# RWKV time mixing on one core: batch 11 wholly by the DMA crossbar, stores held back between the crossbar blocks, and reordered ends

## The chip, the cores and the metric

One NeuronCore of a Trainium2 chip runs the kernel. Its engines are TensorE (PE), VectorE (DVE), ScalarE (ACT), GpSimd (POOL) and SyncE (SP), which here only issues DMAs; sixteen DMA engines move the data. The metric is device time in microseconds, lower is better.

## The reference

`x` is 16 batches x 2048 steps x 256 channels in float32. The three token-shift mixes are formed, but `k` isn't used by the output:

```python
x_prev[:, 1:, :] = x[:, :-1, :]
xv = x * time_mix_v + x_prev * (1 - time_mix_v)
xr = x * time_mix_r + x_prev * (1 - time_mix_r)
v = xv.reshape(-1, d_model) @ value_weight
r = xr.reshape(-1, d_model) @ receptance_weight
out = (1 / (1 + exp(-r)) * v).reshape(-1, d_model) @ output_weight
```

## The kernel before

The rows are cut into 64 units of 512 rows, four per batch; `g` counts units (0 to 63). Channels lie in two blocks of 128 (`ko`). Everything on the way is bf16; PSUM and the output are float32.

**Data in.** POOL's DMA queue loads a batch at a time and casts it to bf16 (`load`, L109), some five batches ahead; the last one, batch 15, is issued at `g` = 34. A batch's rows stand as 16 rows per partition, so that the row before slot `j` is slot `j - 1`, and only slot 0 needs the last slot shifted by one partition: the "wrap copy" (L408 on VectorE, in `wrap_slots`; L522 on ScalarE for the last batches). The first two batches are laid out unit by unit (`xt_first`), so there every unit has its wrap copy.

**Transposes.** The projections need channels on the partitions. For units up to 45 TensorE transposes (`transposes`, L200: eight 128 x 128 transposes a unit) and ScalarE copies PSUM to `xt` (L216). This runs up to `LOOK` = 6 units ahead of the unit that is computed (`advance`). The last `BYDMA` = 18 units are transposed by the DMA crossbar instead (`by_dma`, L181, issued on SyncE's queue): two quarters of batch 11 at `g` = `CROSS` = 40, batch 12 at 41, 13 at 43, 14 at 47 and 15 at 51. The first of these waits for the last load. Of batch 11 the units 44 and 47 are still TensorE's.

**Mixing.** The time-mix coefficients are folded into the weights, so a mix is one product and one add: `mix = c * x_prev + x`. VectorE or ScalarE forms the product of channel block 0 (`scale`, L249; `scale_act`, L491), POOL that of block 1 (`scale_pool`, L259), VectorE adds (`add`, L271). From unit 10 on a product covers two units. From `g` = `FREE` = `CROSS` on ScalarE takes block 0 of the value mix from VectorE.

**Unit g, in order.** TensorE projects receptance (`psum_r`), ScalarE takes the sigmoid to `s_sb` (L512); transposes of a later unit; TensorE projects value (`psum_v`, L279); VectorE multiplies to `z_sb` (L549); TensorE projects the output of unit `g - 1` (`psum_o`, L303), which ScalarE copies to `o_sb` (L335). From `g` = 41 (`LATE_O`) the output that is projected is that of `g - 2`, before the value. `psum_r`, `psum_v` and `psum_o` hold one buffer each, of two PSUM banks; `ps_t` has two buffers.

**Data out.** Two units are stored together, 1 MB, on SyncE's queue (`store`, L313; L338 for the first two batches), in the order in which the program names them: a store behind a crossbar transfer waits for its issue. `o_sb` and `xt` have three buffers of a batch each, `x_bf` six.

**The ends.** At the start TensorE runs 21 matmuls on zeros (L144), then the first units' transposes from float32; one-off work on weights runs beside. At the end units 60 to 62 are put out in halves (`out_part`), and `last_unit` takes unit 63 by halves and its output by quarters.

The order of issue is written out by hand: an engine runs its instructions in the program's order, and `add_manual_dep` adds a wait where data alone doesn't.

Of the kernel before, what the change touches and what calls it, by code (L numbers as in the profile page):

```python
# [15 lines left out]
def kernel(  # L16
# [38 lines left out]
    BYDMA = 4 * UB + 2  # L55
    CROSS = NU - BYDMA - LOOK
    FREE = CROSS
    LATE_O = CROSS
    START_T = [1, 3, 5, 6, 7, 9, 11, 12]
    AHEAD = 6  # L60
    PAIRS = 10
    WARM = 21
# [16 lines left out]
    late_copies = []  # L79
    x_bf = {}  # L80
# [5 lines left out]
    zeros = consts.tile([P, P], BF16)  # L86
# [13 lines left out]
    def load(b):  # L100
        if b not in x_bf:
            x_bf[b] = xpool.tile([P, J, D], BF16, name="x_bf")
        if b < BYUNIT:
            for e in range(UB):
                nc.gpsimd.dma_start(
                    out=x_bf[b][:, e * UJ : (e + 1) * UJ, :], in_=unit_rows(x, b, e)[:, 0]
                )
            return
        return nc.gpsimd.dma_start(out=x_bf[b], in_=rows(b), max_dma_last_dim=8192)  # L109
# [31 lines left out]
    def warm_up(n):  # L141
        ps = ps_t_pool.tile([P, P], FP32, name="ps_t")
        for _ in range(n):
            nc.tensor.matmul(out=ps, lhsT=zeros, rhs=zeros, start=True, stop=True)  # L144

    warm_up(WARM)

# [70 lines left out]
    def first_transposes():  # L218
        def half(h, pool, name):
            ps = pool.tile([P, UJ, KO, P], FP32, name=name)  # L220
            for jj in range(H):
                for ko in range(KO):
                    nc.tensor.transpose(
                        out=ps[:, jj, ko],
                        in_=x_unit[:, 0, h * H + jj, ko * P : (ko + 1) * P],
                        identity=ident_f,
                    )
            if h == 1:
                nc.vector.tensor_copy(out=xt[0][:, 0, :, 1:P], in_=ps[:, H - 1, :, 0 : P - 1])
            nc.scalar.copy(out=xt[0][:, 1 + h * H : 1 + h * H + H], in_=ps[:, 0:H])  # L230

        half(1, ps_r_pool, "psum_r")
        half(0, ps_v_pool, "psum_v")
# [77 lines left out]
    def store(queue, b, lo, hi):  # L311
        dst = out[b].rearrange("(p j) d -> p j d", p=P)
        queue.dma_start(out=dst[:, lo:hi, :], in_=o_sb[b][:, lo:hi, :])  # L313
# [9 lines left out]
    def output(g, z):  # L323
        b, e = divmod(g, UB)
        if e == 0:
            o_sb[b] = opool.tile([P, J, D], FP32, name="o_sb")
        j0 = e * UJ
        if g >= NU - 4:
            for h, (pool, name) in enumerate([(ps_t_pool, "ps_t"), (ps_o_pool, "psum_o")]):
                out_part(pool, name, z, b, e, h * H, H, nc.scalar.copy, nc.sync)  # L330
            return
        ps = ps_o_pool.tile([P, UJ, D], FP32, name="psum_o")
        for jj in range(UJ):
            out_matmuls(ps, z, jj, jj)
        nc.scalar.copy(out=o_sb[b][:, j0 : j0 + UJ, :], in_=ps)  # L335
        if b < BYUNIT:
            if e % 2 == 1:
                nc.sync.dma_start(  # L338
                    out=unit_rows(out, b, e - 1, 2),
                    in_=o_sb[b][:, j0 - UJ : j0 + UJ, :].rearrange("p (e j) d -> p e j d", j=UJ),  # L340
                )
        elif g >= NU - 8:
            store(nc.sync, b, j0, j0 + UJ)
        elif e % 2 == 1:
            store(nc.sync, b, j0 - UJ, j0 + UJ)

    def last_unit(g):
# [10 lines left out]
        for h, (lo, hi) in enumerate(cols):  # L358
            project(banks[h], g, 0, lo, hi)
            nc.scalar.activation(out=s_sb[:, :, lo:hi], in_=banks[h], func=ACT.Sigmoid)  # L360
        def value(h):
            lo, hi = cols[h]
            project(banks[2 + h], g, 1, lo, hi)
            nc.vector.tensor_tensor(
                out=z_sb[:, :, lo:hi], in0=s_sb[:, :, lo:hi], in1=banks[2 + h], op=ALU.mult
            )

        def before(h):
            pool, name = [(ps_o_pool, "psum_o"), (ps_r_pool, "psum_r")][h]
            out_part(pool, name, z_prev, b, e - 1, h * H, H, by_act, nc.sync)  # L370

        before(0)
        value(0)
        before(1)
        value(1)
        out_part(ps_v_pool, "psum_v", z_sb, b, e, 0, 1, by_act, nc.sync)
        out_part(ps_o_pool, "psum_o", z_sb, b, e, 1, 1, by_dve, nc.sync)
# [14 lines left out]
    def wrap_slots(piece, one=None):  # L392
# [15 lines left out]
        nc.vector.tensor_copy(  # L408
            out=xt[b][:, j, kos, 1:P], in_=xt[b][:, j + n, kos, 0 : P - 1]
        )  # L410

    tnext = 1
    last_load = None

    def advance(limit):
        nonlocal tnext, last_load
        while tnext <= min(limit, NU - 1):
# [3 lines left out]
            elif b > 1 and e == 0 and b + 5 < B:  # L421
                if b == 2:
                    load(6)
                last_load = load(b + 5)
            if tnext < NU - BYDMA:
                transposes(tnext)
# [27 lines left out]
    warm_up(WARM2)  # L454
# [44 lines left out]
    for g in range(NU - 1):  # L499
# [13 lines left out]
        if g == CROSS:  # L513
            for e in (1, 2):
                by_dma(B - 5, e * UJ, (e + 1) * UJ, last_load)
        advance(START_T[g] if g < len(START_T) else g + LOOK - (g == CROSS - 1))
        for b in range(B - 4, B):
            if g == max(UB * (b - 2) - 1, CROSS + 1):
                new_xt(b)
                by_dma(b, 0, J)  # L520
# [20 lines left out]
        for p in pooled[g]:  # L541
            wrap_slots(p)
# [6 lines left out]
        nc.vector.tensor_tensor(out=z_sb, in0=s_sb, in1=ps_v, op=ALU.mult)  # L549
        for p in pooled[g]:  # L550
            scale_pool(p, last)
# [38 lines left out]
```

## Time and profile before

| | |
|---|---|
| median of 4 runs | 203.65 us (203.1 to 204.22) |
| the profiled execution | 203.96 us, its span 202.2 us |
| TensorE, VectorE, ScalarE, POOL busy | 97%, 92%, 90%, 41% |
| DMA packets under 512 B | 19716 of 31130 |
| SyncE's queue q1, POOL's queue q0: share of 16 DMA engines | 59.3%, 40.1% |
| HBM read, written | 34.34 MB, 33.55 MB: 336 GB/s over the span |

The span runs from the first to the last recorded event; the profiled execution took 1.76 us more. An engine's busy time says how much of the span it worked, not that it set the end. A line such as L303 is a line of the kernel; a helper's line stands for all its callers, and the tile's name tells them apart. "SPq" is SyncE's queue: its time is that in which a DMA is issued, not the transfer's own.

### The profile page before, as it was taken

The page shows a single profiled execution, that of the slowest core. Times are in us where ns is not written, and L with a number is a line of the kernel's source. Part 1 is how long each engine was busy: PE and PEld are TensorE (multiplying, and loading weights), DVE is VectorE, ACT ScalarE, POOL GpSimd, SP SyncE. Part 2 cuts the span into 40 slices and gives each one's busy share as a digit, 9 for nine tenths or more (in the row PEclk, how much of TensorE's full clock was granted, in tenths as well). Part 3 has the DMA queues.
Part 4 walks back from the last instruction along what each step waited for, and adds up shares of the span by engine and source line. Part 5 has one row for each costly group of instructions (what it writes and reads, how often), then busy time and mean ns, then how long its engine had stood idle before and what let it go on. Part 6 is the DMA issues. An engine that isn't in the chain of part 4 may idle for free.

```text
span 202.2 us, 3922 instructions
## 1 busy us (share of the span) xinstructions
PE 196.0 (97%) x1436; PEld 126.9 (63%) x1436; DVE 186.8 (92%) x301; ACT 181.1 (90%) x202; POOL 83.6 (41%) x109
## 2 busy tenths in 40 slices
PE   7989999999999999999999999999999999999992
PEld 6756676666666666666666666655656565655671
DVE  3789999999999999999999999999999999999963
ACT  2699999999999999999999999989999999999982
POOL 1646353443443634425453443434344444444200
PEclk9999999999999999999999999999999999999999
DMA  5999999999999999999999999999999999987575
GB/s 164 290 147 216 230 280 276 275 283 273 292 309 314 315 312 305 301 315 290 286 302 293 299 302 301 297 337 222 293 164 389 230 365 220 329 363 313 211 309 210
DMA packets 31130, 56.74 MB, mean 281 GB/s; under 512 B 19716, under 2 KB 21000, under 8 KB 28040
## 3 DMA queue, kind: packets, MB, share of 16 engines
q1 hardware_dynamic: 26160, 40.24, 59.3%
q0 software_dynamic: 4800, 16.12, 40.1%
q8 instruction: 11, 0.18, 0.3%
q10 hardware_dynamic: 152, 0.13, 0.2%
q14 instruction: 7, 0.06, 0.1%
HBM read 34.34 MB, written 33.55 MB: 336 GB/s over the span
## 4 chain that ended last, share of the span: by engine, by line
PE 77%; DVE 6%; ACT 5%; DMA 5%; issue 4%; SPq 0%; POOL 0%; DVEq 0%; ACTq 0%
PE psum_o L303 24%; PE psum_v L279 23%; PE psum_r L279 22%; PE ps_t L200 7%; DMA x_bf<-in_x_dram 3%; DMA w_f<-n_receptance_weight_dram 2%; DVE mix L271 2%; ACT s_sb L512 2%; DVE mix L249 2%; ACT o_sb L335 2%; ACT mix L491 1%; DVE z_sb L549 1%; PE ps_t L303 1%; ACT xt L216 1%; ACT xt_first L216 0%
## 5 line engine op out<-in xcount | busy, mean ns | idle before, releaser
L259 POOL TENSOR_SCALAR mix<-xt,c_sb 128x1024 bf16<-128x1024 bf16 (+1 forms) x55 | 61.2, 1112 | 91.6 <-DVE mix L271 83.2
L549 DVE TENSOR_TENSOR z_sb<-s_sb,psum_v 128x1024 bf16<-128x1024 bf16 x63 | 76.6, 1216 | 3.7 <-PE psum_v L279 1.5
L271 DVE TENSOR_TENSOR mix<-mix,xt 128x1024 bf16<-128x1024 bf16 x112 | 77.2, 697 | 1.7
L279 PEld LDWEIGHTS <-w_bf 128*128 128x128 bf16 x516 | 48.7, 98 | 37.9 <-issue 0.8
L512 ACT ACTIVATE s_sb<-psum_r 128x1024 bf16<-128x1024 f32 x63 | 65.0, 1031 | 3.4 <-PE psum_r L279 2.7
L335 ACT COPY o_sb<-psum_o 128x1024 f32<-128x1024 f32 x60 | 61.1, 1018 | 7.6 <-PE psum_o L303 7.5
L279 PE MATMUL psum_v<-mix,w_bf 128*128 128x512 bf16 (+1 forms) x256 | 65.3, 377 | 0.3 <-DVE z_sb L549 0.2
L303 PE MATMUL psum_o<-wo_bf,z_sb 128*128 128x256 bf16 x494 | 64.4, 272 | 0.1
L279 PE MATMUL psum_r<-mix,w_bf 128*128 128x512 bf16 (+1 forms) x252 | 64.2, 377 | 0.1
L303 PEld LDWEIGHTS <-z_sb 128*128 128x128 bf16 x512 | 49.9, 98 | 20.7 <-issue 1.5
L216 ACT COPY xt<-ps_t 128x1024 bf16<-128x1024 bf16 x38 | 38.6, 1027 | 0.0
L200 PEld LDWEIGHTS <-x_bf 128*128 128x128 bf16 x344 | 22.5, 98 | 10.3 <-POOL xt_first L407 1.3
L200 PE MATMUL ps_t<-ident,x_bf 128*128 128x128 bf16 x344 | 25.7, 219 | 0.8 <-DMA x_bf<-in_x_dram 0.8
L249 DVE TENSOR_SCALAR mix<-xt,c_sb 128x1024 bf16<-128x1024 bf16 (+1 forms) x50 | 22.5, 458 | 0.0
L491 ACT ACTIVATE mix<-xt,c_sb 128x1024 bf16<-128x1024 bf16 x11 | 12.7, 1157 | 0.0
L109 POOL DMA_DIRECT2D x_bf<-in_x_dram x14 | 10.5, 752 | 0.0
L271 DVE TENSOR_TENSOR mix<-mix,xt_first 128x1024 bf16<-128x1024 bf16 x15 | 10.2, 684 | 0.1
L259 POOL TENSOR_SCALAR mix<-xt_first,c_sb 128x512 bf16<-128x512 bf16 x6 | 4.2, 697 | 8.7 <-DVE xt_first L408 8.7
L249 DVE TENSOR_SCALAR mix<-xt_first,c_sb 128x512 bf16<-128x512 bf16 x22 | 6.7, 353 | 0.2
L216 ACT COPY xt_first<-ps_t 128x1024 bf16<-128x1024 bf16 x5 | 5.1, 1028 | 0.4 <-PE ps_t L200 0.4
L144 PE MATMUL ps_t<-zeros 128*128 128x128 bf16 x31 | 3.7, 313 | 1.0 <-DVE zeros L87 1.0
L144 PEld LDWEIGHTS <-zeros 128*128 128x128 bf16 x31 | 3.3, 149 | 1.0 <-DVE zeros L87 1.0
(64 smaller groups left out, 48.2 us busy)
## 6 DMA issues: line engine op xcount, KB each, us to landing
out_dram<-o_sb SPq DMA_DIRECT2D x28, 1024.0 KB, 9.5
x_bf<-in_x_dram POOLq DMA_DIRECT2D x14, 1024.0 KB, 26.4
out_dram<-o_sb SPq DMA_DIRECT2D x4, 512.0 KB, 2.7
out_dram<-o_sb SPq DMA_DIRECT2D x6, 256.0 KB, 2.5
x_bf<-in_x_dram POOLq DMA_DIRECT2D x5, 256.0 KB, 7.3
o_sb<-in_x_dram SPq DMA_DIRECT2D x2, 512.0 KB, 5.0
o_sb<-in_x_dram SPq DMA_DIRECT2D x2, 256.0 KB, 3.2
out_dram<-o_sb SPq DMA_DIRECT2D x3, 128.0 KB, 2.0
```

Source lines behind the costliest of these rows:

```text
L109: return nc.gpsimd.dma_start(out=x_bf[b], in_=rows(b), max_dma_last_dim=8192)
L200: nc.tensor.transpose(out=ps[:, jj], in_=src[:, jj, ko * P : (ko + 1) * P], identity=idn)
L216: nc.scalar.copy(out=xt[b][:, j0 : j0 + UJ], in_=ps)
L249: nc.vector.tensor_scalar(out=mixed(piece)[:, :, ko], in0=xt[b][:, slots(piece), ko], scalar1=c_sb[:, m, ko : ko + 1], scalar2=None, op0=A ...
L259: op = nc.gpsimd.tensor_scalar(out=mixed(piece)[:, :, 1], in0=xt[b][:, slots(piece), 1], scalar1=c_sb[:, m, 1:2], scalar2=1.0, op0=ALU.mul ...
L271: return nc.vector.tensor_tensor(out=mixed(piece), in0=mixed(piece), in1=xt[b][:, slots(piece, 1)], op=ALU.add)
L279: nc.tensor.matmul(out=ps[:, mo, :], lhsT=w_bf[:, m, ko, mo * P : (mo + 1) * P], rhs=mixed((b, m, e * TU + lo, e * TU + hi))[:, :, ko], st ...
L303: nc.tensor.matmul(out=ps[:, slot, :], lhsT=z[:, ko, jj * P : (jj + 1) * P], rhs=wo_bf[:, ko, :], start=(ko == 0), stop=(ko == KO - 1),)
L335: nc.scalar.copy(out=o_sb[b][:, j0 : j0 + UJ, :], in_=ps)
L491: nc.scalar.activation(out=mixed(piece)[:, :, ko], in_=xt[b][:, slots(piece), ko], func=ACT.Copy, scale=c_sb[:, m, ko : ko + 1],)
L512: nc.scalar.activation(out=s_sb, in_=ps_r, func=ACT.Sigmoid)
L549: nc.vector.tensor_tensor(out=z_sb, in0=s_sb, in1=ps_v, op=ALU.mult)
```

## The change

- The crossbar takes 20 units: all of batch 11, in four pieces (last quarter first), at `g` = 38, then batch 12 at 39. `CROSS`, `LATE_O` and `FREE` fall from 40 to 38 by this. ScalarE makes batch 11's wrap copy.
- `WAITING` names five stores that are put into SyncE's queue later: the one that follows unit 33 at `g` = 38, 35 at 39, 39 at 43, 45 and 47 at 51. The first of them waits for half of the last load, and the crossbar for the whole of it.
- Batch 15 is loaded by two DMAs, one for each half.
- Batch 1's wrap copies move to POOL, behind the unit's last add.
- The warm-up runs 5 matmuls of 512 columns; the first PSUM copy of ScalarE stands before VectorE's.
- Units 60 and 61 put out both halves through `ps_t`. Unit 62's product for `z_sb` comes in two halves. In `last_unit` the order of the work changes, VectorE makes one of the copies that ScalarE made and the other way round, and the product of the second half is cut in two.

```diff
-    BYDMA = 4 * UB + 2
+    BYDMA = 5 * UB
     CROSS = NU - BYDMA - LOOK
     FREE = CROSS
     LATE_O = CROSS
+    WAITING = {33: 38, 35: 39, 39: 43, 45: 51, 47: 51}
...
-    WARM = 21
+    WARM = 5
...
-    zeros = consts.tile([P, P], BF16)
+    zeros = consts.tile([P, TU], BF16)
...
-        return nc.gpsimd.dma_start(out=x_bf[b], in_=rows(b), max_dma_last_dim=8192)
+        if b < B - 1:
+            return nc.gpsimd.dma_start(out=x_bf[b], in_=rows(b), max_dma_last_dim=8192)
+        return [
+            nc.gpsimd.dma_start(out=x_bf[b][:, j : j + J // 2], in_=rows(b)[:, j : j + J // 2])
+            for j in (0, J // 2)
+        ]
...
+            nc.scalar.copy(out=xt[0][:, 1 + h * H : 1 + h * H + H], in_=ps[:, 0:H])
             if h == 1:
                 nc.vector.tensor_copy(out=xt[0][:, 0, :, 1:P], in_=ps[:, H - 1, :, 0 : P - 1])
-            nc.scalar.copy(out=xt[0][:, 1 + h * H : 1 + h * H + H], in_=ps[:, 0:H])
...
+    def store(queue, b, lo, hi, after=None):
         dst = out[b].rearrange("(p j) d -> p j d", p=P)
-        queue.dma_start(out=dst[:, lo:hi, :], in_=o_sb[b][:, lo:hi, :])
+        op = queue.dma_start(out=dst[:, lo:hi, :], in_=o_sb[b][:, lo:hi, :])
+        if after is not None:
+            tc.add_manual_dep(op.ins, after.ins.name, SYNC, reason="in turn with the last load")
...
         if g >= NU - 4:
-            for h, (pool, name) in enumerate([(ps_t_pool, "ps_t"), (ps_o_pool, "psum_o")]):
-                out_part(pool, name, z, b, e, h * H, H, nc.scalar.copy, nc.sync)
+            for h in range(2):
+                out_part(ps_t_pool, "ps_t", z, b, e, h * H, H, nc.scalar.copy, nc.sync)
...
         elif e % 2 == 1:
-            store(nc.sync, b, j0 - UJ, j0 + UJ)
+            pair = (b, j0 - UJ, j0 + UJ)
+            if g in WAITING:
+                kept.setdefault(WAITING[g], []).append(pair)
+            else:
+                store(nc.sync, *pair)
...
+        def value(h, n):
             lo, hi = cols[h]
             project(banks[2 + h], g, 1, lo, hi)
...
+            for c in range(lo, hi, n * P):
+                nc.vector.tensor_tensor(
...
-        before(0)
-        value(0)
-        before(1)
-        value(1)
+        receptance(0)
+        out_part(ps_o_pool, "psum_o", z_prev, b, e - 1, 0, H, by_dve, nc.sync)
+        receptance(1)
+        value(0, H)
+        out_part(ps_r_pool, "psum_r", z_prev, b, e - 1, H, H, by_act, nc.sync)
+        value(1, 1)
         out_part(ps_v_pool, "psum_v", z_sb, b, e, 0, 1, by_act, nc.sync)
-        out_part(ps_o_pool, "psum_o", z_sb, b, e, 1, 1, by_dve, nc.sync)
+        out_part(ps_o_pool, "psum_o", z_sb, b, e, 1, 1, by_act, nc.sync)
...
-        nc.vector.tensor_copy(
+        op = (nc.vector if after is None else nc.gpsimd).tensor_copy(
             out=xt[b][:, j, kos, 1:P], in_=xt[b][:, j + n, kos, 0 : P - 1]
         )
+        if after is not None:
+            tc.add_manual_dep(op.ins, after.ins.name, SYNC, reason="one at a time")
...
-        if g == CROSS:
-            for e in (1, 2):
-                by_dma(B - 5, e * UJ, (e + 1) * UJ, last_load)
         advance(START_T[g] if g < len(START_T) else g + LOOK - (g == CROSS - 1))
-        for b in range(B - 4, B):
-            if g == max(UB * (b - 2) - 1, CROSS + 1):
+        for b in range(B - 5, B):
+            if g == max(UB * (b - 2) - 1, CROSS + (b > B - 5)):
                 new_xt(b)
-                by_dma(b, 0, J)
+                if b == B - 5:
+                    for pair in kept.pop(g):
+                        store(nc.sync, *pair, after=half_load)
+                    for e in (3, 0, 1, 2):
+                        by_dma(b, e * UJ, (e + 1) * UJ, last_load)
+                else:
+                    by_dma(b, 0, J)
+                for pair in kept.pop(g, []):
+                    store(nc.sync, *pair)
             if g == UB * (b - 1) + 1:
                 nc.scalar.copy(out=xt[b][:, 0, :, 1:P], in_=xt[b][:, J, :, 0 : P - 1])
...
         for p in pooled[g]:
-            wrap_slots(p)
+            if p[0] != 1:
+                wrap_slots(p)
...
-        nc.vector.tensor_tensor(out=z_sb, in0=s_sb, in1=ps_v, op=ALU.mult)
+        n = TU // 2 if g == NU - 2 else TU
+        for c in range(0, TU, n):
+            nc.vector.tensor_tensor(
...
         for p in pooled[g]:
+            wrap_slots(p, after=last)
             scale_pool(p, last)
```

## The prediction

> **What bounds the kernel now.** I read the page first, then the chain of waits over 120 to 165 us, then busy time by stretches, then SyncE's own timeline, and last the timelines of the two ends.
>
> The page: one core, TensorE busy nearly throughout.
>
> ```profile
> span 202.2 us, 3922 instructions
> PE 196.0 (97%) x1436; PEld 126.9 (63%) x1436; DVE 186.8 (92%) x301; ACT 181.1 (90%) x202; POOL 83.6 (41%) x109
> ```
>
> A busy PE says little by itself, so the chain of waits in order of time (start, us, what) has to show that one unit follows another on TensorE:
>
> ```profile
> 124.67 0.86 PE psum_r L279 x4
> 125.53 0.45 PE ps_t L200 x8
> 125.98 0.86 PE psum_v L279 x4
> 126.84 0.87 PE psum_o L303 x8
> ...
> 148.85 0.86 PE psum_r L279 x4
> 149.72 1.01 PE psum_o L303 x8
> 150.73 0.86 PE psum_v L279 x4
> ```
>
> Up to unit 40 a unit is 0.86 + 0.45 + 0.86 + 0.87 = 3.04 us. After it the 0.45 us of transposes is gone: 2.60, and 0.14 more once per batch (the 1.01). From 138.26 (unit 42) to 185.65 (unit 60) that is 47.39 / 18 = 2.633 a unit.
>
> The crossbar must deliver on time, so the DMA's pace counts. Busy time by stretches (PE, PEld, DVE, ACT, POOL, then clock, DMA share, GB/s): stores alone, a crossbar batch, and one that took longer:
>
> ```profile
> 152.50:157.50 5.00, 5.00 (x33) 2.94 (x32) 4.90 (x8) 4.55 (x6) 2.01 (x4) 1.00 1.04 393
> 157.60:162.60 5.00, 5.00 (x32) 2.92 (x30) 4.97 (x8) 4.89 (x7) 1.98 (x3) 1.00 1.09 223
> 168.00:174.10 6.10, 6.10 (x40) 3.78 (x39) 6.08 (x9) 5.99 (x8) 3.08 (x3) 1.00 1.21 178
> ```
>
> So a 1 MB store takes about 2.6 us of all DMA engines, a crossbar batch (four units) 5.0 to 6.1 us; the two slow ones each held an instruction fetch. SyncE's timeline shows who queues behind whom:
>
> ```profile
> 131.84 0.33 SPq L313 DMA_DIRECT2D out_dram<-o_sb  x1
> 133.99 7.76 SPq L181 DMA_TRANSPOSE xt<-x_bf  x3
> ...
> 152.10 9.30 SPq L181 DMA_TRANSPOSE xt<-x_bf  x1
> ```
>
> The first crossbar transfer waited for the last load until 133.99. One issue then holds SyncE for up to 9.3 us, and stores stand behind it.
>
> **The change part by part.**
>
> **Two more units by the crossbar.** Removed from TensorE: 2 x 8 transposes, 2 x 0.45 = 0.90 us, all on the path. ScalarE loses two PSUM copies (2 x 1.03). Added on ScalarE: batch 11's wrap copy (0.41 us, the L522 row); its four siblings now each delay the psum_o copy and cost TensorE the 0.14 above, so I charge 0.14. VectorE loses its own 0.21 us copy for that. Unit 40's product for value moves from VectorE to ScalarE (1.16 us, L491) two units earlier, with the stall around 138.0 (about 0.3 us) that the same order causes now: moved, not added. Sum: **-0.76** (-0.90 if the wrap is free, -0.62 if it costs twice).
>
> **Is the data there?** POOL moves 4 KB load packets at 197 GB/s when alone (109 to 111 us: 0.39 MB by its queue) and about half that beside stores. At 120 us there were 1.45 MB of loads left. With two 1 MB stores kept back they need 1.45 / 0.197 = 7.3 us: load 15 ends near 127.9 and lands near 129 instead of 133.9. The store of units 32+33 goes between its halves. Then SyncE's queue runs, by the rows above (5.25 us a batch): batches 11+12 130 to 140.7; two stores to 146; batch 13 to 151.5; three stores to 159.5; batches 14+15 to 171, or 172 with a fetch. ScalarE reads each batch's last slot in its wrap copy (148.32 for batch 12 now; 10.5 us later for each following). Due, 1 us earlier than now: batch 11's first piece 136.8 (lands 133), batch 13 at 157.8 (152.5), batch 14 at 168.3 (166), batch 15 at 179 (172). All in time, the nearest by 2 us; ScalarE's in-order queue would stand still if not. The kept stores free their output buffers in time too: units 44 to 47 are stored by about 177 and unit 56's copy writes there at 181. Cost **0**; if late, see the rivals.
>
> Under the Trainium skill ("Advanced Engine Details and Errata", X-Bar Transpose) crossbar transfers are as fast as ordinary ones; this trace has 5.0 to 6.1 us against 2.6 for the same bytes. By the rule two units would cost the queue about 1.3 us, an estimate.
>
> By the rows they cost it 2.5 to 3.1 us.
>
> **Last load in halves.** One more issue on POOL (0.75 us, L109) at 116.1; POOL's next product starts at 117.80 after 0.66 idle, so it slips by 0.1, and VectorE adds that product a unit later: 0. If that cover were gone, 0.75.
>
> **Start.** Warm-up of 5 x 512 columns for 21 x 128: 2.42 us now is 115 ns for 128 columns, so 5 x 0.43 to 0.46 = 2.2 us, the same. The memset grows by some 0.1 us. The swapped order of the first copies: VectorE's waits 0.6 us longer, then still stands idle until 6.32. All of this is covered: the chain lies in DMAs until 13.11. If the clock opened later, TensorE's 1.3 us idle before 13.08 is the cover.
>
> Four wrap copies of batch 1 go from VectorE to POOL. The start's timeline:
>
> ```profile
> 21.51 0.22 DVE L408 COPY xt_first<-xt_first 128x254 bf16<-128x254 bf16 x1
> 21.64 1.21 DVE L549 TENSOR_TENSOR z_sb<-s_sb,psum_v 128x1024 bf16<-128x1024 bf16 x1
> ...
> 33.97 1.02 PE L279 MATMUL psum_v<-mix,w_bf 128*128 128x512 bf16 x4 [0.24 <-DVE z_sb L549]
> ```
>
> VectorE is the bound there: it runs without a gap from 18.38 to 33.9. A copy costs 0.13 start to start, and the first of the four stands before a wait for ScalarE, so 3 x 0.13 = 0.40. TensorE's gaps that VectorE makes are 0.16, 0.19 (before 20.26 and 23.51) and 0.40 (before 33.97). After 34 TensorE runs without gaps, so what is gained stays. POOL's copy I estimate at 0.47 us (0.69 for 512 elements and 1.12 for 1024 give 0.26 + 0.84 ns each); it waits for the add, and the product behind it is read a unit (3 us) later. A VectorE add beside POOL's work took 0.80 instead of 0.68 (134.06), so four copies could give back 0.4. I take **-0.3** (bounds +0.4 and -0.75).
>
> The Trainium skill ("SBUF — State Buffer", SBUF: two separate sides) speaks against this: VectorE and GpSimd hold a shared port pair as an exclusive lock. If each POOL copy blocked VectorE fully, the start would be an estimated 4 x 0.47 - 0.4 = 1.5 us slower.
>
> The 0.12 us row above is what I go by.
>
> **Tail.** Its timeline:
>
> ```profile
> 190.49 1.02 ACT L335 COPY o_sb<-psum_o 128x1024 f32<-128x1024 f32 x1
> ...
> 191.56 0.60 PE L303 MATMUL psum_o<-wo_bf,z_sb 128*128 128x256 bf16 x4
> ...
> 197.49 0.69 DVE L364 TENSOR_TENSOR z_sb<-s_sb,ps_t 128x512 bf16<-128x512 bf16 x1 [0.18 <-PE ps_t L279]
> 198.24 0.61 PE L303 MATMUL ps_t<-wo_bf,z_sb 128*128 128x256 bf16 x4 [0.26 <-DVE z_sb L364]
> ...
> 198.89 0.42 DVE L320 COPY o_sb<-ps_t 128x256 f32<-128x256 f32 x1 [0.37 <-PE ps_t L303]
> ```
>
> Unit 60's second half waited 0.28 us for psum_o's copy; in the other ps_t buffer it doesn't: -0.28, and TensorE runs on to the last value matmul at about 196.95 instead of 197.23. Unit 62 by halves keeps that: its output half starts at 194.75, its z half is done at 194.5, while a whole z would be ready at 195.1. The last product in two (0.42 each by the 256-column copy row, instead of one of 0.69) lets column block 2 go out before 3; block 3's product ends 0.16 us nearer to the last matmul. VectorE's new copy of 512 columns (0.69) ends at 196.1, before the product at 196.25. Sum **-0.44** (bounds +0.15, if that copy comes in the way, and -0.7).
>
> **Sum.** -0.76 - 0.3 - 0.44 = -1.5 us. Profiled execution: 203.96 us (span 202.2 and 1.76 around it) becomes 202.46, span 200.7. The runs' median is 203.65, 0.31 below the profiled one: **202.15**.
>
> **The rivals.**
>
> *Only TensorE's share arrives.* Start and tail give nothing (POOL beside VectorE, copies in the way): -0.76, 202.9. For it: VectorE is 92% busy and the tail is a net of short steps; against: the gaps named above have one visible cause each. 0.19.
>
> *The crossbar queue runs late: slower.* If load 15 lands at 133.9 as now, because its pace isn't set by the stores, the whole line moves 4 us: block one ends 144.7, batch 13 at 155.5, batch 14 at 168 to 170, landing a microsecond later. ScalarE's wrap copy at 168.3 stands 0.6 to 2.6 us and holds TensorE. Then 10 MB of stores are left from 173 to 176: 26 us, to 199 to 202, and 2.2 us to the end: span 201.3 to 204.2. Middle 203.2, so 204.65. The point: in the forecast the stores end near 197.5 + 2.2 = 199.7, 1 us before the span's end; each microsecond beyond that is paid in full, and from 3.5 us late the kernel is slower. For it: the queue is refilled without pause until 181 us even now; against: 197 GB/s for loads alone stands in the trace. 0.16.
>
> *Late by 2 us only* (a fetch in each block): the last stores eat 1 us: 203.1. 0.08.
>
> **How the numbers follow.** 0.57 for the forecast, 202.15 (its own range 201.4 to 202.6). 0.5% is 1.0 us, about what a measurement here can tell. Faster by more: 0.57. Within it, 0.19 + 0.08 = 0.27. Slower 0.16. Low 201.4 is about -0.90 - 0.65 - 0.7; high 204.5 takes in most of the slower rival; about 0.15 is left out.
>
> **What would show it.** L200's bf16 transposes 344 to 328, L216 copies of xt two fewer, no unit of 3.04 us after unit 38; L181 issues from about 129, not 134 (the step most in doubt); no ScalarE wait for a DMA before the wrap copies (L522); stores idle before the last ones; no 0.40 gap near 34 us and none of 0.28 at 191. A first crossbar issue after 132, or ScalarE waiting for xt, would prove me wrong.

## The result and the profile after

| | before | after |
|---|---|---|
| median of the runs | 203.60 us (79 runs) | 203.23 us (53 runs) |
| ratio after to before | | 0.9978 (95%: 0.9967 to 0.9990) |
| the profiled execution | 203.96 us, span 202.2 | 204.63 us, span 202.9 |

The change makes the kernel 0.4 us faster, not the 1.5 us forecast. The interval of the ratio lies below 1, but the gain is under the 1.0 us (0.5%) that the prediction named as about what a measurement here can tell. After's profiled execution is one of the longest of its kernel (202.51 to 204.63 us), so spans can't be compared. What can is pieces of the timeline, cut at the sigmoids (ScalarE's first work on a unit). Two profiled executions of after agree within 0.03 us on every piece from unit 3 to the last store's issue.

| us, from the traces | before | after | after, second execution |
|---|---|---|---|
| start to sigmoid 3 | 20.02 | 20.90 | 20.00 |
| sigmoid 3 to 8 | 16.80 | 16.89 | 16.86 |
| 8 to 20 | 37.01 | 37.01 | 37.01 |
| 20 to 44 (the middle) | 70.73 | 69.94 | 69.93 |
| 44 to 59 | 39.80 | 39.80 | 39.79 |
| 59 to the last store's issue | 14.99 | 14.56 | 14.56 |
| issue to its last byte landed | 1.94 | 2.50 | 2.21 |
| landed to the end of the span | 0.94 | 1.27 | 1.29 |

The middle gave -0.79 and the tail -0.43 up to the last issue, as forecast; from sigmoid 3 to 8 the start gave nothing, and behind the last issue 0.6 to 0.9 us were given back. Now the views.

The page of after, its head and the rows of the transposes and their copies:

```profile
span 202.9 us, 3861 instructions
PE 196.7 (97%) x1404; PEld 125.4 (62%) x1404; DVE 187.4 (92%) x297; ACT 180.2 (89%) x202; POOL 85.6 (42%) x114
L225 ACT COPY xt<-ps_t 128x1024 bf16<-128x1024 bf16 x36 | 36.5, 1027 | 0.0
L209 PE MATMUL ps_t<-ident,x_bf 128*128 128x128 bf16 x328 | 24.5, 219 | 0.0
```

TensorE has 32 instructions fewer (16 transposes, and 16 matmuls of the warm-up); transposes fell from 344 to 328 as listed. The chain of waits of after (start, us, what), at the last transposes and later at two wrap copies:

```profile
122.59 0.86 PE psum_r L288 x4
123.46 0.45 PE ps_t L209 x8
123.90 0.88 PE psum_v L288 x4
...
138.53 0.86 PE psum_r L288 x4
139.39 0.98 PE psum_o L312 x8
140.37 0.86 PE psum_v L288 x4
...
148.17 0.86 PE psum_v L288 x4
149.03 0.86 PE psum_r L288 x4
149.90 1.01 PE psum_o L312 x8
```

The 0.45 us of transposes leave two units sooner: from sigmoid to sigmoid a unit takes 3.05 us up to unit 37 in after, up to unit 39 in before. The wrap copy of batch 11, now ScalarE's, delays one more psum_o: 0.98 at 139.39 instead of 0.87, so it costs 0.11 where 0.14 was charged, and 0.90 less 0.11 is the 0.79 measured. (The 1.01 at 149.90 belongs to batch 12 and stands in before too, at 149.72.) SyncE's timeline shows whether the data was there:

```profile
126.33 0.33 SPq L322 DMA_DIRECT2D out_dram<-o_sb  x1
128.93 11.25 SPq L190 DMA_TRANSPOSE xt<-x_bf  x5
140.29 1.01 SPq L322 DMA_DIRECT2D out_dram<-o_sb  x2
141.59 9.38 SPq L190 DMA_TRANSPOSE xt<-x_bf  x1
...
154.79 14.63 SPq L190 DMA_TRANSPOSE xt<-x_bf  x2
```

The first kept store goes out between the load's halves, the first crossbar issue stands at 128.93 (forecast 129; 133.99 before). The transfers themselves ran at 130.2 to 141.6, 146.7 to 151.8 and 160.0 to 170.8, against 130 to 140.7, to 151.5 and to 171 or 172. No ScalarE wait for a DMA is listed after 120 us.

The tail, from after's timeline:

```profile
191.03 1.04 PE L312 MATMUL ps_t<-wo_bf,z_sb 128*128 128x256 bf16 x8
...
195.58 0.69 DVE L331 COPY o_sb<-psum_o 128x512 f32<-128x512 f32 x1 [0.27 <-PE psum_o L312]
...
197.40 0.75 DVE L383 TENSOR_TENSOR z_sb<-s_sb,ps_t 128x256 bf16<-128x256 bf16 x2 [0.19 <-PE ps_t L288]
...
198.64 0.42 DVE L331 COPY o_sb<-ps_t 128x256 f32<-128x256 f32 x1 [0.49 <-PE ps_t L312]
```

The stand of 0.28 us for psum_o is gone, VectorE's new copy ends before the product, and the last product comes in two (0.75 together). All as forecast; yet the end of the kernel did not come sooner by as much.

### The profile page after: what moved, and what is told of

It reads as the page before. It is cut to its first block, busy times and chain, and to the rows that moved or that the text cites. A ratio compares the mean times of both kernels' runs of the same rounds, so it can differ in the third digit from the quotient of the medians.

```text
span 202.9 us, 3861 instructions
## 1 busy us (share of the span) xinstructions
PE 196.7 (97%) x1404; PEld 125.4 (62%) x1404; DVE 187.4 (92%) x297; ACT 180.2 (89%) x202; POOL 85.6 (42%) x114
## 4 chain that ended last, share of the span: by engine, by line
PE 80%; DVE 8%; ACT 5%; issue 3%; DMA 2%; SPq 0%; DVEq 0%
PE psum_v L288 23%; PE psum_o L312 23%; PE psum_r L288 22%; PE ps_t L209 7%; DVE z_sb L581 3%; DVE mix L280 3%; DVE mix L258 2%; ACT s_sb L536 2%; DMA o_sb<-in_x_dram 2%; PE psum_r L302 1%; PE ps_t L312 1%; ACT mix L515 1%; ACT xt_first L225 1%; PE psum_v L232 1%; PE ps_t L151 1%
## 5 line engine op out<-in xcount | busy, mean ns | idle before, releaser
L581 DVE TENSOR_TENSOR z_sb<-s_sb,psum_v 128x1024 bf16<-128x1024 bf16 (+1 forms) x64 | 76.6, 1199 | 3.1 <-PE psum_v L288 1.3
L312 PE MATMUL psum_o<-wo_bf,z_sb 128*128 128x256 bf16 x486 | 63.2, 272 | 0.0
L312 PEld LDWEIGHTS <-z_sb 128*128 128x128 bf16 x512 | 49.8, 98 | 20.5 <-issue 1.4
L225 ACT COPY xt<-ps_t 128x1024 bf16<-128x1024 bf16 x36 | 36.5, 1027 | 0.0
L209 PEld LDWEIGHTS <-x_bf 128*128 128x128 bf16 x328 | 21.5, 98 | 8.8
L209 PE MATMUL ps_t<-ident,x_bf 128*128 128x128 bf16 x328 | 24.5, 219 | 0.0
L258 DVE TENSOR_SCALAR mix<-xt,c_sb 128x1024 bf16<-128x1024 bf16 (+1 forms) x49 | 22.0, 458 | 0.0
L515 ACT ACTIVATE mix<-xt,c_sb 128x1024 bf16<-128x1024 bf16 x12 | 13.9, 1156 | 0.0
L112 POOL DMA_DIRECT2D x_bf<-in_x_dram x13 | 9.8, 754 | 0.0
L151 PE MATMUL ps_t<-zeros 128*128 128x128 bf16 (+1 forms) x15 | 3.6, 419 | 1.2 <-DVE zeros L89 1.2
L218 ACT CAST xt_first<-ps_t 128x512 bf16<-128x512 f32 x4 | 2.2, 586 | 2.7 <-PE ps_t L209 2.6
```

Source lines behind the costliest of these rows:

```text
L209: nc.tensor.transpose(out=ps[:, jj], in_=src[:, jj, ko * P : (ko + 1) * P], identity=idn)
L225: nc.scalar.copy(out=xt[b][:, j0 : j0 + UJ], in_=ps)
L258: nc.vector.tensor_scalar(out=mixed(piece)[:, :, ko], in0=xt[b][:, slots(piece), ko], scalar1=c_sb[:, m, ko : ko + 1], scalar2=None, op0=A ...
L312: nc.tensor.matmul(out=ps[:, slot, :], lhsT=z[:, ko, jj * P : (jj + 1) * P], rhs=wo_bf[:, ko, :], start=(ko == 0), stop=(ko == KO - 1),)
L515: nc.scalar.activation(out=mixed(piece)[:, :, ko], in_=xt[b][:, slots(piece), ko], func=ACT.Copy, scale=c_sb[:, m, ko : ko + 1],)
L581: nc.vector.tensor_tensor(out=z_sb[:, :, c : c + n], in0=s_sb[:, :, c : c + n], in1=ps_v[:, :, c : c + n], op=ALU.mult,)
```

## The experiments

The times called landing and end are those of the table. Unless said otherwise a ratio is to the kernel before, from runs on the same chip.

**1. Where the end went: the turn of the semaphores.** Theory: SyncE's DMAs take eight semaphores in turn, and at the end SyncE waits for them in a fixed order, 0.06 us each. Two more DMAs (batch 11 in four pieces instead of two) move the last store from the last place in that order to the second, so that the waits behind it come after its landing. The rival is that the longer end belongs to the new tail. SyncE's waits over the last 8 us (what for: us in total, times, longest) of before:

```profile
SPq L585 <- DMA out_dram<-o_sb: 1.1, 4, 0.4
```

and of after:

```profile
SPq L623 <- DMA out_dram<-o_sb: 2.0, 2, 1.3
```

Before, four waits end one by one as the last stores land. After, the second wait lasts until the last landing, and six more follow it, 0.06 us apart. Two kernels test it:

```diff
 # after, batch 11 in two transfers
-                    for e in (3, 0, 1, 2):
-                        by_dma(b, e * UJ, (e + 1) * UJ, last_load)
+                    for lo, hi in ((3 * UJ, J), (0, 3 * UJ)):
+                        by_dma(b, lo, hi, last_load)
 # before, with two more DMAs of 1 KB at the start
+    spare_in = consts.tile([2 * KO, P], FP32)
+    for m, tm in enumerate([time_mix_r, time_mix_v]):
+        nc.sync.dma_start(out=spare_in[m * KO : (m + 1) * KO, :], in_=...)
```

> The changed kernel, batch 11 by the crossbar in two transfers instead of four (last quarter, then the other three quarters). Two DMAs fewer on SyncE's queue, so the last store of all takes another of the eight semaphores in turn. Theory of the end: SyncE waits for the DMAs' semaphores in a fixed order with one instruction of 0.06 us each, and in the changed kernel the last store sits on the second of eight, so that six or seven waits follow its landing (201.58 to 202.03); with two DMAs fewer it sits on the eighth. Then the time is 0.4 us less than the changed kernel's 203.23 (202.8), and one wait follows the last landing. Rival (the end's 0.95 us is a late landing alone): no change, 203.2. If three quarters in one transfer land too late for POOL: a wait for the DMA at unit 41 or 42, up to 1 us more.

> The kernel before with two extra DMAs of 1 KB on SyncE's queue at the start, into a tile that nobody reads: everything else is as before, but the last store moves from the eighth to the second semaphore in turn. Theory of the end: 0.4 us slower than before (204.0 against 203.6), six waits of 0.06 us after the last landing. Rival (the order of semaphores costs nothing): 203.6.

Measured: in two transfers, landing to end 0.90 instead of 1.27, with the middle's 69.94 kept; ratio 0.998 (0.9956 to 1.0004). The 0.4 us expected against after doesn't show in these times (after has 0.9978): in this execution the landing took 2.59 us, for the reason of experiment 3. The kernel before with two idle DMAs: 1.29 instead of 0.94, with every other piece from sigmoid 8 on unchanged; ratio 1.0036 (1.0014 to 1.0058), whose interval holds the 0.35 us (1.0017). In its waits the same pattern, without any of the change:

```profile
SPq L590 <- DMA out_dram<-o_sb: 1.5, 2, 1.2
```

So 0.35 us of the loss is the turn, shown by the traces from both sides.

**2. The warm-up and the wrap copies, each put back.** The first has the 21 matmuls of 128 columns again, the second leaves batch 1's wrap copies on VectorE.

```diff
 # after, old warm-up
-    WARM = 5
+    WARM = 21
-    warm_up(WARM, TU)
+    warm_up(WARM)
 # after, wrap copies on VectorE
-            if p[0] != 1:
-                wrap_slots(p)
+            wrap_slots(p)
...
-            wrap_slots(p, after=last)
```

> The changed kernel with the warm-up of before (21 matmuls of 128 columns, small zero tile). In the profiled execution of the changed kernel TensorE's full clock was granted at 10.15 us, in that of the kernel before at 6.94, and units start about 1 us later by 34 us. Theory A (the new warm-up makes the late clock more frequent): the median falls by 0.3 to 0.6 us to 202.7 to 202.9. Rival B (the clock is granted on a grid of its own whose phase differs from execution to execution, whatever the warm-up): the median stays at 203.2, with the same spread of some 1.5 us.

> The changed kernel with batch 1's wrap copies on VectorE again. Theory: POOL's copy pushes POOL's product under VectorE's add, which takes 0.80 instead of 0.68 us, so the 0.13 us saved per unit is given back: no change (203.2, within 0.15). By my prediction the move was worth 0.3: then 203.5. Rival (shared port lock): 202.9.

Measured: with the wraps back on VectorE, sigmoid 3 to 8 took 16.94 us, 0.05 more than in after. That is within the spread: 16.79 to 16.96 in the traces with these copies on VectorE, 16.80 to 17.01 with them on POOL. So the pieces show no gain from the move. The timed runs don't decide: the ratio was 1.0 (0.9974 to 1.0026), the median 203.67, nearer to the 203.5 of a gain of 0.3 than to 203.2, but the interval overlaps that of after. Why stands in the timelines. Before (VectorE and POOL, the unit whose wrap copy is at 21.51):

```profile
21.90 0.69 POOL L259 TENSOR_SCALAR mix<-xt_first,c_sb 128x512 bf16<-128x512 bf16 x1 [1.66 <-DVE xt_first L408]
...
22.77 0.68 DVE L271 TENSOR_TENSOR mix<-mix,xt_first 128x1024 bf16<-128x1024 bf16 x1
```

After:

```profile
22.45 1.21 DVE L581 TENSOR_TENSOR z_sb<-s_sb,psum_v 128x1024 bf16<-128x1024 bf16 x1
22.66 0.40 POOL L428 COPY xt_first<-xt_first 128x254 bf16<-128x254 bf16 x1 [1.14 <-DVE mix L280]
23.15 0.69 POOL L268 TENSOR_SCALAR mix<-xt_first,c_sb 128x512 bf16<-128x512 bf16 x1
...
23.58 0.80 DVE L280 TENSOR_TENSOR mix<-mix,xt_first 128x1024 bf16<-128x1024 bf16 x1
...
34.94 1.02 PE L288 MATMUL psum_v<-mix,w_bf 128*128 128x512 bf16 x4 [0.24 <-DVE z_sb L581]
```

Before, POOL's product ran beside VectorE's z product, which reads PSUM and kept its 1.21 us. Now it starts 0.4 us later in the unit, behind the copy, and its end lies under the start of the add, which goes from 0.68 to 0.80. The add waits for POOL's product to end: it ends 0.54 us after that one (24.38 and 23.84), and so does every add of before and after in whose way POOL's product stands, by 0.06 us or more past VectorE's operation ahead of the add (0.535 to 0.543 us, 74 adds). The longest shows it best:

```profile
49.63 1.12 POOL L268 TENSOR_SCALAR mix<-xt,c_sb 128x1024 bf16<-128x1024 bf16 x1 [2.27 <-PE psum_o L312]
...
50.14 1.15 DVE L280 TENSOR_TENSOR mix<-mix,xt 128x1024 bf16<-128x1024 bf16 x1
```

VectorE saves 0.13 us of copy and pays 0.12 in the add; z products follow each other after 3.26 us in both (21.64 and 24.90 before, 22.45 and 25.71 after). TensorE's wait of 0.24 for z is still there.

With the old warm-up the ratio was 0.9969 (0.9945 to 0.9993), and the trace differed at the other end of the kernel: landing 2.11 instead of 2.50 (2.21). That led to the next group.

**3. The instruction fetch.** A 16 KB fetch on the instruction queue (q8) holds one DMA engine for about a microsecond. In after it starts 4.0 us ahead of the last store's issue, among the last stores; with the old warm-up 7.9 us ahead, in before 10.1. Theory: its place follows from TensorE's instruction count. The test adds only tiny instructions:

```diff
     warm_up(WARM, TU)
+    warm_up(16, 8)
```

> The changed kernel with 16 more matmuls of eight columns behind its five at the start, so that TensorE has as many instructions as with the old warm-up, and nothing else changes. Theory (the place of the 16 KB instruction fetch near the end follows from TensorE's instruction count): the fetch moves from 4.0 us to about 7.8 us ahead of the last store issue, the last store lands 2.0 to 2.1 us after its issue instead of 2.2 to 2.5, SyncE's issues near the end take 0.33 us, sigmoid of unit 59 to the end 17.9 us instead of 18.1 to 18.3; ratio to the kernel before 0.996 to 0.998. Rival (it was the old warm-up itself, by the clock at the start): the fetch stays at 4.0 us, and the end stays 18.1 to 18.3 us.

Measured: the fetch moved to 8.0 us ahead, landing 2.11, sigmoid 59 to end 17.96 (18.33 and 18.06 without the dummies), ratio 0.9962 (0.9929 to 0.9995). The DMA rows of three microseconds near the end, of after:

```profile
q1 hardware_dynamic: 421, 0.76, 67.4%
q8 instruction: 1, 0.02, 1.9%
issues: line engine op xcount, KB each, median us to landing
out_dram<-o_sb SPq DMA_DIRECT2D x3, 256.0 KB, 3.3
```

and of the kernel with the dummies, the same place:

```profile
q1 hardware_dynamic: 516, 0.96, 83.2%
issues: line engine op xcount, KB each, median us to landing
out_dram<-o_sb SPq DMA_DIRECT2D x3, 256.0 KB, 2.1
```

No q8 row, and the 256 KB stores land after 2.1 us instead of 3.3: in after the last of the sixteen shares of each arrives 0.8 to 1.3 us behind the other fifteen. The delay shrinks from store to store but reaches the last one. The rival, an effect of the warm-up on the clock, falls for this part, since the warm-up was after's.

**4. Three drops: does the queue before the last unit bind?** From the traces I had read that the last landing comes some 3.7 us after the issue of unit 62's second store whatever else was done, and took this for the DMA engines' pace. So that store (0.25 MB) was left out of three kernels: after; after with two transfers and the old warm-up; before. Each kernel of this experiment ran once.

```diff
-        store(queue, b, lo, lo + n)
+        if (b, lo) != (B - 1, 2 * UJ + H):
+            store(queue, b, lo, lo + n)
```

> The changed kernel without the store of unit 62's second half (0.25 MB of the output is not written). Theory (the last landing is set by the DMA engines' work in the queue, some 0.36 MB/us, not by the time of the last store alone): the last landing comes about 0.5 us sooner after the last issue, 1.7 to 2.0 instead of 2.2 to 2.5 us. Rival (what follows the last issue is the latency of that store): 2.2 to 2.5 us as with the store.

> The changed kernel with batch 11 in two transfers and the old warm-up, without the store of unit 62's second half (0.25 MB of the output is not written). Theory (the DMA engines' pace binds): the last landing 1.5 to 1.8 us after the last issue instead of 2.08 to 2.10. Rival (the last store's own latency): 2.1 us as with the store.

> The kernel before without the store of unit 62's second half (0.25 MB of the output is not written). Theory (the pace binds here too, though its last issue comes 0.43 us later against the rest of the queue): landing 1.5 to 1.8 us after the last issue instead of 1.94; if it stays at 1.94, that is the latency of the last store alone, and only the changed kernels are bound by the pace.

Measured, landing after the last issue: 2.08 for after (2.50 and 2.21 with the store); 2.07 for the second (2.08 and 2.10); 1.93 for before (1.94). Where no fetch is near, 0.25 MB less moved nothing, so the theory of the pace fell. After's landing fell to 2.08 with the fetch still at 4.0: the fetch costs by a backlog, and with less in the queue it is worked off before the last store.

That leaves 0.15 us: without a fetch the new tail lands after 2.07 to 2.11, the old one after 1.93 to 2.01. New theory: the last unit's own four quarters crowd each other, since the tail issues the last three within 0.57 us instead of 0.73 (all four within 0.99 instead of 1.15, so 0.16 closer). The first quarter's store was left out (the same edit, with `3 * UJ` as its row).

> The changed kernel with batch 11 in two transfers and the old warm-up, without the store of unit 63's first quarter (0.13 MB of the output is not written). Leaving out 0.25 MB of unit 62 moved nothing (2.07 against 2.08), so the queue before the last unit does not bind. New theory (the last unit's own quarters, issued 0.19 us closer together than before, take turns on the DMA engines): with one quarter less the last landing comes 1.93 to 1.98 us after the last issue, as in the kernel before. Rival (a store issued in that place takes 2.1 us by itself): 2.07 to 2.11 as with the quarter.

> The kernel before without the store of unit 63's first quarter (0.13 MB of the output is not written). Both theories: the quarters do not crowd each other here, so the last landing stays 1.90 to 1.95 us after the last issue; if it falls below 1.85, the quarters take turns here too and the floor of one store lies lower than assumed.

Measured: 1.88 with the new tail, 1.91 with the old. With one quarter less the new tail has no handicap, which fits quarters that crowd each other. Leaving one out did two things, though: less was moved, and the next quarter was issued 0.15 us sooner (13.84 instead of 13.99), so that the last three were 0.72 apart as in before. Which of the two counts isn't shown. From the first quarter's issue to the last landing it is 3.06 to 3.16 us with either tail when no fetch is near, but for 3.32 in the tail alone (experiment 5). The tail issues that quarter only 0.27 us sooner, and by this reading that, not 0.43, is its worth.

**5. Parts of the change alone.** The middle alone (loads, stores and crossbar of after; start and tail of before), the tail alone (on the kernel before), the middle without its kept stores (all else of after), and the new warm-up alone (on the kernel before):

```diff
 # after without kept stores
-    WAITING = {33: 38, 35: 39, 39: 43, 45: 51, 47: 51}
+    WAITING = {}
```

> The kernel before with the crossbar's part alone: 20 units, stores held back, last load in halves; start and end of before. My step of -0.76 us for the middle: the sigmoid of unit 44 comes 69.9 us after that of unit 20 (70.73 before). Theory of the end: 0.35 us of it are given back because the last store sits on the second semaphore, and some 0.1 by the fetch (some 6 us ahead of the last store): 203.25. Rival (the loss is all in the tail's own reordering): 202.8, with 0.94 us after the last landing.

> The kernel before with the new tail alone (units 60 and 61 through ps_t, unit 62 and the last unit rearranged). The count of DMAs and of TensorE's instructions is that of before, so neither the semaphores' turn nor the fetch moves. Theory: the last store is issued 14.56 us after unit 59's sigmoid instead of 14.99, it lands 1.94 to 2.1 us later, 0.94 us follow: 203.15 to 203.3, all of the step of -0.44. Rival (the tail's stores crowd each other, so the landing is later whatever the fetch): landing 2.4 to 2.6 us after the issue, 203.6.

> The changed kernel with no store held back (nothing waits for half of the last load). The first crossbar transfer is issued near 134 instead of 129. By the prediction's slower rival: the whole line moves by 4 to 5 us, ScalarE waits for batch 11 or batch 14, 0.5 to 1.5 us slower than the changed kernel (203.7 to 204.7). If holding back is worth nothing: 203.2 and the first issue at 129 all the same.

> The kernel before with the new warm-up alone: 32 TensorE instructions fewer, so the last instruction fetch moves from 10 to about 6.2 us ahead of the last store. Theory: the end stays as in the kernel before (17.87 to 18.0 us from unit 59's sigmoid), since the fetch is still 4 us ahead of unit 62's stores; the start alone could change. Theory A (the new warm-up opens the clock later): 0.3 us slower, 203.9, and a grant after 5 us. Rival B (the grant is a matter of phase alone): 203.6.

| | ratio (95%) | 20 to 44 | 59 to issue | landing | end |
|---|---|---|---|---|---|
| middle alone | 0.9993 (0.9968 to 1.0019) | 69.94 | 14.99 | 2.01 | 1.29 |
| tail alone | 0.9996 (0.9979 to 1.0014) | 70.73 | 14.56 | 2.33 | 0.90 |
| no kept stores | 1.0068 (1.0041 to 1.0095) | 70.26 | 14.56 | 2.34 | 1.28 |
| warm-up alone | 0.9989 (0.9965 to 1.0013) | 70.73 | 14.99 | 1.93 | 0.91 |

The middle alone has its -0.79 and its four pieces' 0.35 at the end. The tail alone landed 2.33 us after its issue in this execution, 0.39 later than before and between what theory and rival expected. The last 16 KB fetch was 9.6 us ahead; but of the last store's sixteen shares one arrived at 2.33 us, the others by 2.07, and an 8 KB fetch on another instruction queue (q14) ran from 1.73 to 2.36 us after the issue (in before one starts at 3.49, after the landing). Whether that fetch is the cause isn't shown. The timed runs tell neither of the two from the kernel before. With the new warm-up alone the 16 KB fetch lay 8.4 us ahead of the last issue, not 6.2 as expected: the same 32 instructions that move it by about 4 us in after moved it by 1.6 us here. Without kept stores the first crossbar issue is late, as SyncE's timeline of that kernel shows:

```profile
120.10 6.42 SPq L322 DMA_DIRECT2D out_dram<-o_sb  x2
132.43 10.49 SPq L190 DMA_TRANSPOSE xt<-x_bf  x5
...
165.03 9.24 SPq L190 DMA_TRANSPOSE xt<-x_bf  x1
```

3.5 us later than 128.93. Batches 11 and 12 are through at 144.3 instead of 141.6, batch 13 at 154.9 instead of 151.8, and batch 15, the last, at 175.7 instead of 170.8; batch 14 is not late (it landed at 165.7 instead of 166.4). This is close to the prediction's slower rival, and it is slower, by 0.9% against after (six runs). Two things differ, though: the first issue, and the order of the stores between the later blocks. The trace places 0.32 us of the loss in the middle piece. Some 0.4 us more lies outside the span: all six runs took 2.1 to 2.3 us beyond it, those of after 1.73 to 1.95. The rest I could not place. The mechanism that the rival named, ScalarE standing at the wrap copy, does not show in that execution: no ScalarE wait for a DMA is listed.

**6. The version that the runs point to.** After with batch 11 in two transfers (no turn lost) and the old warm-up (the fetch away from the end); run twice, beside a second run of after. Then the same with the output half of unit 62 moved ahead of the last value and copied by VectorE:

```diff
-        value(0, H)
-        out_part(ps_r_pool, "psum_r", z_prev, b, e - 1, H, H, by_act, nc.sync)
+        out_part(ps_r_pool, "psum_r", z_prev, b, e - 1, H, H, by_dve, nc.sync)
+        value(0, H)
```

> The changed kernel with both suspects of the end undone: batch 11 in two crossbar transfers (the last store takes the eighth semaphore in turn again) and the warm-up of before (32 TensorE instructions more, which puts the last 16 KB instruction fetch 7.9 us ahead of the last store instead of 4.0). Theory of the end: after the last landing 0.90 us as in the kernel before (1.27 in the changed kernel), from the last store's issue to its landing 2.0 to 2.1 us (2.50), so 0.7 to 0.8 us less than the changed kernel: 202.5. Rival (the start's spread from execution to execution decides the medians and the end nothing): 203.2.

> The changed kernel with batch 11 in two transfers and the warm-up of before, once more beside the changed kernel on one chip. Theory: 0.8 us faster than the changed kernel, all of it after unit 59 (17.54 us against 18.2 to 18.4): 202.4, clear of the kernel before by about 1 us. If the first result was the luck of the start, it comes out at 202.8 to 203.2.

> The changed kernel itself, beside the next two on one chip. From unit 59's sigmoid to the end 18.2 to 18.4 us (17.87 in the kernel before): store issue 14.56, landing 2.3 to 2.6 with the instruction fetch 4.0 us ahead of the last store, 1.27 after it. Unit 44's sigmoid 69.94 us after unit 20's. Median 203.2. If the new warm-up opens the clock later as a rule, the grant comes after 5 us again (5.2, 5.8, 7.1, 10.2 in four executions; 4.2 to 6.9 in six with the old one).

> As the kernel with two transfers and the old warm-up, but the second output half of unit 62 goes out ahead of the last unit's first value projection and VectorE copies it, so its store is issued some 0.5 us earlier. In every execution without a late fetch the last landing came 3.67 to 3.75 us after the issue of that store, whatever the order of the rest: 0.75 MB leave at the DMA's pace. Theory (the DMA's pace binds the end): the last landing comes 0.2 to 0.4 us earlier though the last store is issued up to 0.2 us later: 202.1. Rival (the last store's own issue binds): 0.2 us slower, 202.6.

Measured: 0.9952 (0.9929 to 0.9975) and 0.9953 (0.9928 to 0.9979); after, again, 0.9973 (0.9944 to 1.0003). These are the lowest ratios of all, 1.0 us below the kernel before, but the intervals overlap those of after and of the kernels of experiments 2 and 3. The medians were 202.41 and 203.00, against 203.67 and 203.58 for before and 203.32 for after: the second lies where it was expected if the first was the luck of the start. What repeats is the piece: sigmoid 59 to the end 17.54 and 17.56 us, against 18.33 and 18.06 in after. Its waits at the end are again resolved one by one:

```profile
SPq L621 <- DMA out_dram<-o_sb: 1.3, 3, 0.8
```

The further edit gave 0.9969 (0.9945 to 0.9993), no better: VectorE's copy delays the product for TensorE, and the last issue comes at 15.07 instead of 14.56:

```profile
196.54 0.39 PE L310 MATMUL psum_v<-wo_bf,z_sb 128*128 128x256 bf16 x2 [0.51 <-DVE z_sb L381]
```

## Why the prediction was wrong

Two steps failed: the start's gain of 0.3 us didn't come, and the sum had no term for what lies behind the last store's issue, where 0.6 to 0.9 us were given back.

- **Two units by the crossbar, -0.76: right.** -0.79, in every kernel that has them with the stores kept back.
- **Is the data there, 0: right**, to within 1 us on every block. (By the sum's own terms load 15 ends near 127.4, not 127.9.) A crossbar batch alone took 5.1 us (146.7 to 151.8), against 2.6 for a store of the same bytes. Leaving the stores in their old order cost 0.9%, so the change needs this step, though by which wait isn't shown.
- **Start, -0.3: wrong, 0.** The bound was named (adds of 0.80 instead of 0.68 could give back 0.4), and it is what happened: three of the four adds took 0.80, the fourth 0.70. I took a value between the ends instead. What I missed is that the copy on POOL pushes POOL's own next product from under an operation that it doesn't disturb to under one that it does. The exclusive lock of the Trainium skill ("SBUF — State Buffer", SBUF: two separate sides) has conditions that I left out: one of its cases is a VectorE operation with two SBUF inputs against a POOL operation that reads SBUF. The traces agree with that case: such an add ended 0.54 us after POOL's product, however long it had to stand (1.15 us at 50.14). The POOL copies lie beside the z product, whose other input is in PSUM, and which kept its 1.21 us; so the 1.5 us of my estimate didn't arise.
- **Tail, -0.44: right at the last issue (-0.43), wrong as a gain.** The sum put what lies behind that issue at nothing, without a reason. By the pieces it went from 2.88 us (1.94 + 0.94) to 3.77 and 3.50. Of it 0.35 is the turn of the semaphores, caused by the middle's two more DMAs (shown by experiment 1); 0.15 the new tail's own landing, by the crowding of the quarters as far as is known; 0.1 to 0.4 in the two executions of after, and 0.5 in that of experiment 1, the fetch that the shorter instruction stream moved among the last stores (shown by experiment 3).
- **The sum**, from sigmoid 3 on (the start before it differs by execution). -0.79 + 0.09 - 0.43 + 0.89 = -0.24 by the first trace of after; by the second -0.80 + 0.06 - 0.43 + 0.62 = -0.55; measured -0.4. For the best version the same sum is -0.79 + 0.07 - 0.33 = -1.05, measured -1.0.
- **The rivals.** The nearest was that only TensorE's share arrives (202.9): its size is near, its reason half right, since the tail's gain came and was given back elsewhere. (In the slower rival the middle of spans from 201.3 to 204.2 is 202.75, not 203.2.)
- **Warm-up, 0: open.** The start differs by up to 2 us between executions: sigmoid 3 lies at 18.8 to 20.5 us in twelve traces with the old warm-up, at 19.8 to 20.9 in eight with the new. In after's profiled execution TensorE ran the first projection more slowly:

```profile
7.00 1.06 PE L302 MATMUL psum_r<-xt_first,w_prev 128*128 128x512 bf16 x2
```

In before's it took less:

```profile
6.87 0.63 PE L293 MATMUL psum_r<-xt_first,w_prev 128*128 128x512 bf16 x2
```

By the profile the full clock was granted at 10.15 us and 6.94 us in these, but at 5.59 in the second execution of after and at 9.37 in one with the old warm-up. The means differ by 0.5 us, while the timed runs show no loss from the new warm-up alone (0.9989); the runs don't settle it.

## What to carry to other kernels

A gain at the last instruction is a gain only if what lies behind it stays: follow the last store to its landing, and the last landing through the final waits, and ask for each edit whether it changes the number of DMAs or of instructions, since either can move something at the far end of the kernel. When work goes to an idle engine, look at what that engine's next operation will then lie beside, not only at whether it has time. With executions that differ by a microsecond, compare pieces between two fixed events rather than spans.

## What the runs showed of the hardware

- The order of SyncE's final waits was worth 0.35 us: two idle DMAs of 1 KB at the start of the kernel made its end that much longer (1.29 instead of 0.94).
- One 16 KB instruction fetch made the 256 KB stores behind it land after 3.3 instead of 2.1 us, and sixteen matmuls of eight columns at the start moved that fetch by 4.0 us at the end.
- A VectorE add of two SBUF operands that starts under POOL's product ended 0.54 us after that product: 0.80 us instead of 0.68 in the first units, once 1.15. Beside POOL's product or copy, VectorE's product with an operand in PSUM kept its 1.21 us.
